# Order of the first loads and of the norm at the head of a transformer block

## The chip, the cores and the metric

The kernel runs on one core of one Trainium2 chip. The metric is the device time of one execution, in microseconds (us). Engines are named as in the profile: PE is TensorE (PEld its weight loads), DVE is VectorE, ACT is ScalarE, POOL is GpSimd, SP is SyncE, which here only issues transfers.

## The reference

One layer of a diffusion backbone over 512 latent tokens with a prefix of 256 context tokens, model width 2048, all in float32. Cut to what matters here:

```python
mod_l = silu(c) @ w_ada + b_ada              # six vectors of 2048 for the latent tokens
mod_c = silu(c_ctx) @ w_ada + b_ada          # the same for the context tokens
h_l = rms_norm(x, g_mix_norm)   * (1 + sc_a)  + sh_a
h_c = rms_norm(ctx, g_mix_norm) * (1 + csc_a) + csh_a
p_l, p_c = h_l @ w_in, h_c @ w_in            # 3904 columns
# p_l: low-rank queries, keys and values, rotary key, three conv streams
# p_c: only keys and values are used
x = x + gt_a * (group_rms_norm(concat(attention, gated_conv)) @ w_out)
x = x + gt_f * conv_ffn(rms_norm(x, g_ffn_norm) * (1 + sc_f) + sh_f)   # 2048 -> 2 x 5504 -> 2048
return rms_norm(x, g_final)
```

rms_norm divides each token's row by the root of its mean square (plus 1e-6) and multiplies by a gain.

## The kernel before, in words

Activations lie transposed: 16 tiles of 128 features by 512 tokens, `xs[0]` to `xs[15]`. Every float32 product is made of three PE matmuls on a high and a low part of weights and activations (`mm3`, L169 to L172): ACT casts the high part, DVE subtracts to get the low one (`split` L145, `hilo` L297).

**The head (L405 to L416).** SP loads constants and the row c. `silu_rows` (L368) takes an 8 KB row on one partition, spreads it over 128 partitions by a PE matmul with ones, four times 512 columns, and ACT writes Silu of it: `sv` for c, `svc` for c_ctx. The 16 tiles of x are loaded; `add_squares` (L310) has ACT square each and DVE add it to one running sum. Then come the row c_ctx in the same way, the small constants `sm` (biases, gains, conv taps), and `rms` (L293): PE sums the squares over the partitions (L283), ACT and DVE make the reciprocal root (L261, L262), PE spreads it (L267), ACT copies it to `rl` (L290).

**Modulation.** One row block of `w_ada` gives 128 outputs: two halves of 512 KB (`ada_load`, four buffers, so two blocks at a time), each multiplied with half of `sv` and summed by DVE (`dot_v` L212, L216), 1.2 us a half. `prep(j)` does blocks 16+j (scale) and j (shift), multiplies tile j by `rl` (L398), scales and shifts it on ACT (L401) and splits it into `hl[j]`.

**The projection (L525 to L569).** It runs over three chunks of the 16 feature tiles, of 2, 4 and 10 tiles. In each chunk the first six column blocks (weights `rf`, matmuls into `pf`) run tile by tile as tiles become ready; the 25 others (weights `rw`, matmuls into `pp`) follow one by one. The first chunk's sums are copied to `acc`, later ones are added. The tiles of the later chunks are prepared between the column blocks of the earlier ones (`todo`). During the third chunk `ctx_mods` uses `svc` for the context's modulation, and `ctx_stats` the context's norm, whose root is ACT's next use of the Sqrt table.

**What sets the order.** The program is put in order by a planner, engine by engine, with its own model of times; each engine then runs its list in that order. `keep(...)` fixes the order among the marked instructions: in the head all loads that go through `fetch_to` (L130) stay in program order on SP's queue until `ordered` is cleared at L548, and so do the multiplies by `rl` among DVE's marked instructions. The write of `sv` to memory (`sv_d`, L910) is not marked, and the planner puts it early. A load whose buffer is still in use waits, and all that stands behind it on SP's queue waits too.

Of the kernel before, what the change touches and what calls it, by code (L numbers as in the profile page):

```python
# [10 lines left out]
F32 = mybir.dt.float32  # L11
F32R = mybir.dt.float32r
AF = mybir.ActivationFunctionType
ALU = mybir.AluOpType
# [3 lines left out]
P = 128  # L18
D = 2048
T = 512  # L20
C = 256
NK = D // P
# [9 lines left out]
G = 6  # L32
# [28 lines left out]
def block_kernel(ctx, tc, xt, ctxt, ctxn, c, c_ctx, w_ada, small, w_in, w_inc, w_q, w_kv, w_out,  # L61
                 w_out_first, w_up, w_up_first, w_dn0, w_dn1, w_dn2, consts, out):
    nc = tc.nc
    keep = tc.keep_in_program_order
    V, A, G_, PE, SP = nc.vector, nc.scalar, nc.gpsimd, nc.tensor, nc.sync
# [18 lines left out]
    def t2(shape, dt, name):  # L84
        return act.tile(shape, dt, tag="t2", bufs=NT2, name=name)
# [44 lines left out]
    def fetch_to(dst, src):  # L130

        ins = SP.dma_start(dst, src)
        if ordered[0]:
            keep(ins)

    def load(src, n, name):
        nth["raw"] += 1
        if "raw" in spare and nth["raw"] % 3 == 0:
            raw = spare["raw"].tile([P, 2048], F32, tag="raw", bufs=1, name=name)
        else:  # L140
            raw = wp.tile([P, 2048], F32, tag="raw", bufs=2, name=name)
        fetch_to(raw[:, :n], src)
        return raw
# [44 lines left out]
    sm = con.tile([P, SMW], F32, name="sm")  # L188
    kc = kcp.tile([P, KCW], F32, name="kc")
    io = con.tile([P, 2 * P], F32, name="io")  # L190
    ident, ones = io[:, :P], io[:, P:]
# [6 lines left out]
    mod = con.tile([P, 96], F32, name="mod")  # L198
    modc = con.tile([P, 32], F32, name="modc")
    rl = con.tile([P, T], F32, name="rl")  # L200
    rc = rl[:, :C]
    sv = svp.tile([P, D], F32, name="sv")
# [9 lines left out]
    def dot_v(raw, vec, t, dst, nm):  # L212

        col = tiny(2, f"dv{nm}{t}")
        for i, r in enumerate(raw):
            V.scalar_tensor_tensor(out=r, in0=r, scalar=1.0, in1=vec[:, i * 1024:(i + 1) * 1024], op0=ALU.mult, op1=ALU.mult, accum_out=col[:, i:i + 1])  # L216
        total(col, t, dst)
# [48 lines left out]
        for g in range(r.shape[1]):  # L266
            PE.matmul(pb[:, g * P:(g + 1) * P], bc(r[:, g:g + 1], P), ident, start=True, stop=True)  # L267

    def rms_steps(sqs, n, a, width, dst, wait=0, one=False):

        ng = width // P
        if not one:
            both = big("rs")
            ps, pb = both[:, :512], both[:, 512:]
        else:
            ps = sml("rs")
            pb = ps[:, 256:]
        for _ in range(wait):
            yield

        for i, sq in enumerate(sqs):
            for g in range(ng):
                PE.matmul(ps[:, g:g + 1], sq[:, a + g * P:a + (g + 1) * P], ones[:, 0:1], start=i == 0 and g == 0, stop=i == len(sqs) - 1 and g == ng - 1)  # L283
        r = tiny(4, "rr")[:, :ng]
        rsqrt(r, ps[:, :ng], n)
        for _ in range(wait):
            yield
        spread(pb, r)
        if dst is not None:
            A.copy(out=dst[:, a:a + width], in_=pb[:, :width])  # L290
        yield pb[:, :width]

    def rms(sqs, n, width, dst):  # L293
        for _ in rms_steps(sqs, n, 0, width, dst):
            pass

    def hilo(src, n, nm, width=512):  # L297
# [12 lines left out]
    def add_squares(total, x, n, nm, E=None, a=0, new=tmp):  # L310
        c = slice(a, a + n)
        if total is None:
            total = new([P, T], F32, nm + "t")
            A.activation(total[:, c], x, AF.Square)
            return total
        q = tmp([P, T], F32, nm)
        A.activation(q[:, :n], x, AF.Square)
        (E or V).tensor_tensor(out=total[:, c], in0=total[:, c], in1=q[:, :n], op=ALU.add)
        return total
# [43 lines left out]
    with ExitStack() as pa:  # L363
        p_sb = pa.enter_context(tc.tile_pool(name="psb", bufs=1, side="right", reuse_waits="tile"))
        svc = p_sb.tile([P, D], F32, name="svc")
        spare["w"] = p_sb, 1, 5

        def silu_rows(src, dst, nm):  # L368

            row = wp.tile([P, 2048], F32, tag="raw", bufs=2, name=nm)[0:1, :]  # L370
            fetch_to(row, src)
            for g in range(4):
                if g % 2 == 0:
                    both = big(f"{nm}{g}")
                ps = both[:, (g % 2) * 512:(g % 2 + 1) * 512]
                PE.matmul(ps, ones[0:1, :], row[:, g * 512:(g + 1) * 512], start=True, stop=True)
                A.activation(dst[:, g * 512:(g + 1) * 512], ps, AF.Silu)

        def ada_load(t):
            return ada_tiles(p_sb, 4, w_ada[t], f"ada{t}")  # L380

        def ada(t):
            dot_v(ada_load(t), sv, t, mod[:, t:t + 1], "l")

        hl = {}

        def mods(j):
            ada(16 + j)
            ada(j)

        def prep(j):
            mods(j)
# [2 lines left out]
        def modulate(j):  # L395

            xr = xs[j]
            keep(V.tensor_tensor(out=xr, in0=xr, in1=rl, op=ALU.mult))  # L398
            sc = tiny(1, f"sc{j}")
            scale_of(sc, s("g_mix", j), mod[:, 16 + j:17 + j])  # L400
            A.activation(xr, xr, AF.Identity, bias=mod[:, j:j + 1], scale=sc)  # L401
            hl[j] = hilo(xr, T, f"h{j}")


        SP.dma_start(io, consts[:, KCW:])  # L405
        silu_rows(c, sv, "c")
        xs = []
        ssq = None
        for j in range(NK):
            xs.append(t2([P, T], F32, f"xr{j}"))  # L410
            fetch_to(xs[j], xt[:, j * T:(j + 1) * T])
            ssq = add_squares(ssq, xs[j], T, f"xs{j}")
        silu_rows(c_ctx, svc, "cc")
        fetch_to(sm, small)
        rms([ssq], D, T, rl)
        A.copy(out=ones_r, in_=ones)  # L416

        qan, kvl, krl, kvc, krc = [], [], [], [], []
# [78 lines left out]
        def evac(ci, m, ps):  # L497
            if ci == 0:
                acc[m] = t2([P, T], F32, f"acc{m}")
                A.copy(out=acc[m], in_=ps)  # L500
                return
            V.tensor_tensor(out=acc[m], in0=acc[m], in1=ps, op=ALU.add)  # L502
            if ci < 2:
                return
            if m == 3:
                bg.appendleft(low_rank([acc[i] for i in range(4)], "g_q", T, "qa", qan))
            elif m == 5:
                bg.appendleft(low_rank([acc[i] for i in (4, 5)], "g_kv", T, "kl", kvl))
            elif m == 6:
                bg.appendleft(rope_key())  # L510
            elif m >= 9 and m % 3 == 0:
                q = bg if m < 27 else post
                q.append(conv((m - 9) // 3))
                q.append(gn_sum((m - 9) // 3, acc[m]))
                late_bg.append(gn_apply((m - 9) // 3, acc[m]))
# [8 lines left out]
        off = 0  # L524
        for ci, (k0, n) in enumerate(zip(K0, KCH)):  # L525

            pss = first_banks(f"pf{ci}")
            if ci == 2:
                bg.append(ctx_stats())
            for q in range(n):  # L530
                if ci == 0:
                    prep(q)
                elif ci == 2:
                    if q in (2, 4):
                        modulate(13 + q // 2)
                    next(cm)
                    pump(1)
                if q % 2 == 0:
                    raw = load(w_in[:, off:off + 2 * G * P], 2 * G * P, f"rf{ci}{q}")
                    w = blocks(raw, 2 * G, f"wf{ci}{q}")  # L540
                    off += 2 * G * P
                for g in range(G):
                    mm3(pss[g], w[q % 2 * G + g], hl[k0 + q], q == 0, q == n - 1)
            for g in range(G):
                evac(ci, ORDER[g], pss[g])
            if ci == 1:
                fetch_to(kc, consts[:, :KCW])
                ordered[0] = False  # L548
            per, step = max(1, 2048 // (n * P)), max(1, 4 // n)
            for i, m in enumerate(ORDER[G:]):  # L550
                if i % per == 0:
                    k = min(per, len(ORDER) - G - i) * n
                    raw = load(w_in[:, off:off + k * P], k * P, f"rw{ci}_{m}")
                    off += k * P
                if i % step == 0:
                    ws = blocks(raw, min(step, len(ORDER) - G - i) * n, f"w{ci}_{m}", i % per * n)
                w = ws[i % step * n:(i % step + 1) * n]
                ps = bank(f"pp{ci}_{m}")
                for kk in range(n):
                    mm3(ps, w[kk], hl[k0 + kk], kk == 0, kk == n - 1)  # L560
                evac(ci, m, ps)
                for f, j in todo.get((ci, i), []):
                    f(j)
                if ci == 2:
                    for q in range(2 if i % 4 == 0 else 1):
                        next(cm, None)
                    if i >= 5 and i % 2 == 1 and (i - 5) // 2 < CTX_EARLY:
                        bg.append(ctx_prep((i - 5) // 2))
                    pump(2)  # L569
# [7 lines left out]
    with ExitStack() as pb:  # L577
# [194 lines left out]
        for n, st in enumerate(steps):  # L772
# [17 lines left out]
            if pr < 3:  # L790
                f, p_, i = pieces(pr + 1)[n % 8]
# [534 lines left out]
```

## Time and profile before

| | us |
|---|---|
| the three times shown | 2206.82, 2209.21, 7098.56 |
| their median | 2209.21 |
| the profiled execution | 2206.8 |
| its span | 2204.9 |
| PE busy in it | 2149.2 (97%) |
| DVE busy | 1599.0 (73%) |
| ACT busy | 1010.5 (46%) |
| first matmul of the projection | starts at 30.24 |

The third of the times stands apart and is a disturbance of that execution. Times in the profile are counted from the start of the span. In a row of the view in order of time stand the start, the time from the first start to the last end, engine, line, operation, what it writes and reads, how many were merged, and in brackets how long the engine stood before it and for whom. SPq is the issue of a transfer, not its landing.

### The profile page before, as it was taken

The numbers are of one execution on the slowest core, as the hardware profiler recorded it, in microseconds if no ns is written. First come the engines' busy times: TensorE is split into PE (matmuls) and PEld (weight loads), VectorE is DVE, ScalarE is ACT, GpSimd is POOL, SyncE is SP. The second block draws the span as 40 slices with busy tenths as digits, with TensorE's granted clock in tenths as the row PEclk, the third lists the DMA queues.
The fourth block names the chain that finished last, engine by engine and source line by source line (L and its number), as shares of the span: only waits on it lengthen the run. The fifth ranks groups of instructions, "written<-read, shape, count | busy, mean of one in ns | idle before, by whom it ended". The sixth has DMA issues, their size and how long they took to land.

```text
span 2204.9 us, 34542 instructions
## 1 busy us (share of the span) xinstructions
PE 2149.2 (97%) x13346; PEld 1914.2 (87%) x13346; DVE 1599.0 (73%) x2493; ACT 1010.5 (46%) x1635; POOL 111.3 (5%) x149
## 2 busy tenths in 40 slices
PE   7899999999999999999999999999999999999998
PEld 4688888878888888899999999999999888888887
DVE  7998887678896848777777777777777873633544
ACT  5523333544452237555554555555554432532444
POOL 0000000000000000011111011111110000000000
PEclk9999999999999999999999999999999999999999
DMA  8989884434469925577777777777776995753462
GB/s 331 344 276 334 275 279 150 144 120 149 158 235 358 331 86 172 132 196 201 204 194 195 201 205 195 194 201 201 201 193 200 350 345 159 247 164 92 160 210 88
DMA packets 144264, 466.75 MB, mean 212 GB/s; under 512 B 16290, under 2 KB 20642, under 8 KB 138082
## 3 DMA queue, kind: packets, MB, share of 16 engines
q1 hardware_dynamic: 125652, 405.03, 54.1%
q0 software_dynamic: 16272, 57.42, 12.8%
q8 instruction: 104, 1.70, 0.3%
q10 hardware_dynamic: 2176, 2.10, 0.3%
q14 instruction: 60, 0.49, 0.1%
HBM read 442.73 MB, written 20.71 MB: 210 GB/s over the span
## 4 chain that ended last, share of the span: by engine, by line
PE 91%; DVE 4%; DMA 2%; ACT 2%; issue 1%; SPq 0%; POOL 0%; DVEq 0%; ACTq 0%
PE d L170 7%; PE d L172 7%; PE d L171 7%; PE pp L170 4%; PE pp L172 4%; PE pp L171 4%; PE o L172 1%; PE o L171 1%; PE o L170 1%; PE uf L170 1%; PE uf L171 1%; PE uf L172 1%; PE of L172 1%; PE pf L171 1%; PE of L170 1%; PE of L171 1%
## 5 line engine op out<-in xcount | busy, mean ns | idle before, releaser
L997 POOL DMA_DIRECT2D u_s<-in_w_up x80 | 68.1, 851 | 416.3 <-DMA u_s<-in_w_up 353.4
L153 ACT CAST w_0h<-rw 128x512 fp32r<-128x512 f32 (+1 forms) x63 | 38.5, 618 | 107.3 <-PE pp L171 65.7
L216 DVE SCALAR_TENSOR_TENSOR ada<-ada,sv 128x1024 f32<-128x1024 f32 x64 | 77.4, 1217 | 4.6 <-DMA ada<-in_w_ada 4.6
L491 DVE SCALAR_TENSOR_TENSOR ada<-ada,svc 128x1024 f32<-128x1024 f32 x64 | 75.9, 1218 | 2.0 <-DMA ada<-in_w_ada 1.8
L238 DVE SCALAR_TENSOR_TENSOR ra<-ra,sv 128x1024 f32<-128x1024 f32 x50 | 59.4, 1216 | 0.0
L154 DVE TENSOR_TENSOR w_0l<-rw,w_0h 128x512 fp32r<-128x512 f32 (+1 forms) x63 | 42.4, 680 | 21.8 <-ACT w_0h L153 21.8
L238 DVE SCALAR_TENSOR_TENSOR ada<-ada,sv 128x1024 f32<-128x1024 f32 x46 | 55.7, 1218 | 2.6 <-DMA ada<-in_w_ada 2.6
L1108 DVE TENSOR_TENSOR u<-u,u 128x1024 f32<-128x1024 f32 x40 | 49.0, 1225 | 1.3
L1107 DVE TENSOR_TENSOR u<-u,u_s 128x1024 f32<-128x1024 f32 x40 | 48.7, 1217 | 0.0
L939 POOL DMA_DIRECT2D y_d<-a x43 | 24.7, 576 | 386.2 <-DVE a L938 376.7
L732 POOL TENSOR_TENSOR gr<-gr,half 128x8 f32<-128x8 f32 x4 | 8.3, 2084 | 641.4 <-DVE mx L684 505.3
L238 DVE SCALAR_TENSOR_TENSOR adl<-adl,sv 128x1024 f32<-128x1024 f32 x32 | 38.8, 1218 | 0.2 <-DMA adl<-in_w_ada 0.2
L683 DVE TENSOR_REDUCE mx<-s 128x1 f32<-128x768 f32 x32 | 30.4, 951 | 8.4 <-PE s L673 8.4
L704 DVE TENSOR_TENSOR ptl<-t,pth 128x384 fp32r<-128x384 f32 x64 | 33.2, 548 | 4.2 <-ACT pth L703 4.2
L502 DVE TENSOR_TENSOR acc<-acc,pp 128x512 f32<-128x512 f32 x50 | 33.9, 678 | 1.9 <-PE pp L172 1.8
L703 ACT CAST pth<-t 128x384 fp32r<-128x384 f32 x64 | 28.5, 488 | 14.3 <-PE t L700 14.1
L936 ACT ACTIVATE g<-g 128x512 f32<-128x512 f32 x43 | 27.2, 633 | 12.1 <-DVE g L930 12.1
L928 ACT ACTIVATE g<-cg,sm 128x512 f32<-128x512 f32 x40 | 32.5, 813 | 0.0
L687 ACT ACTIVATE p<-s,mx 128x768 f32<-128x768 f32 x32 | 29.3, 915 | 6.8 <-DVE mx L684 6.6
L928 ACT ACTIVATE a<-ca,sm 128x512 f32<-128x512 f32 x40 | 32.1, 802 | 0.0
L700 PE MATMUL t<-io,p 128*128 128x128 f32 x192 | 27.5, 274 | 3.7 <-ACT p L687 2.4
L929 DVE SCALAR_TENSOR_TENSOR g<-cg,sm,g 128x511 f32<-128x511 f32 x40 | 29.8, 745 | 0.0
(15580 smaller groups left out, 8734.8 us busy)
## 6 DMA issues: line engine op xcount, KB each, us to landing
ada<-in_w_ada SPq DMA_DIRECT2D x174, 512.0 KB, 6.0
u<-in_w_up SPq DMA_DIRECT2D x120, 512.0 KB, 8.3
u_s<-in_w_up SPq DMA_DIRECT2D x80, 512.0 KB, 4.1
u_s<-in_w_up POOLq DMA_DIRECT2D x80, 512.0 KB, 9.5
d<-in_w_dn SPq DMA_DIRECT2D x86, 384.0 KB, 3.8
y<-y_d SPq DMA_DIRECT2D x129, 256.0 KB, 4.5
ra<-in_w_ada SPq DMA_DIRECT2D x25, 1024.0 KB, 4.8
adl<-in_w_ada SPq DMA_DIRECT2D x32, 512.0 KB, 6.0
```

The lines of the kernel that those rows point to most:

```text
L153: A.copy(out=hi[:, :n], in_=raw[:, a:a + n])
L154: V.tensor_tensor(out=lo[:, :n], in0=raw[:, a:a + n], in1=hi[:, :n].bitcast(F32), op=ALU.subtract)
L170: PE.matmul(ps, w[0], x[0], start=first, stop=False, skip_group_check=on_top)
L171: PE.matmul(ps, w[0], x[1], start=False, stop=False, skip_group_check=on_top)
L172: PE.matmul(ps, w[1], x[0], start=False, stop=last, skip_group_check=on_top)
L216: V.scalar_tensor_tensor(out=r, in0=r, scalar=1.0, in1=vec[:, i * 1024:(i + 1) * 1024], op0=ALU.mult, op1=ALU.mult, accum_out=col[:, i:i + 1])
L238: keep(V.scalar_tensor_tensor(out=r, in0=r, scalar=1.0, in1=svs[i], op0=ALU.mult, op1=ALU.mult, accum_out=lc[:, t % 4:t % 4 + 1] if i else ...
L491: keep(V.scalar_tensor_tensor(out=raw[q], in0=raw[q], scalar=1.0, in1=svc[:, q * 1024:(q + 1) * 1024], op0=ALU.mult, op1=ALU.mult, accum_o ...
L928: A.activation(u, src, AF.Identity, bias=s("fb", m), scale=s("fw", 86 + m))
L997: G_.dma_start(r[-1], src[more], accum_op=ALU.add)
L1107: V.tensor_tensor(out=a11, in0=a11, in1=s1, op=ALU.add)
L1108: V.tensor_tensor(out=a12, in0=a12, in1=a11, op=ALU.add)
```

## The change

Four things move in the head:

- the squares of x are summed by fours: DVE adds within four tiles, and PE sums the four results over the partitions into one accumulator; `rms` takes them one by one as they are made. The number of sums is given as `ns`, since they come from a generator;
- `sm` is loaded before x instead of behind the context's row;
- the context's row is no longer spread by PE: a transfer writes it to all 128 partitions (1 MB instead of 8 KB) after the first chunk's first six column blocks, and ACT takes Silu of it in place, in one pass over 2048 columns, after the second chunk's;
- tile 0's multiplication by `rl` is written right behind the norm, and the first loads are written out: scale block 16, then the first weights `rf00`, then shift block 0. Before, both blocks came ahead of the weights.

```diff
@@ rms_steps, rms
-    def rms_steps(sqs, n, a, width, dst, wait=0, one=False):
+    def rms_steps(sqs, n, a, width, dst, wait=0, one=False, ns=None):
...
-                PE.matmul(ps[:, g:g + 1], sq[:, a + g * P:a + (g + 1) * P], ones[:, 0:1], start=i == 0 and g == 0, stop=i == len(sqs) - 1 and g == ng - 1)
+                PE.matmul(ps[:, g:g + 1], sq[:, a + g * P:a + (g + 1) * P], ones[:, 0:1], start=i == 0 and g == 0, stop=i == (ns or len(sqs)) - 1 and g == ng - 1)
...
@@ ada, modulate
         def ada(t):
-            dot_v(ada_load(t), sv, t, mod[:, t:t + 1], "l")
+            dot_v(first.pop(0) if first else ada_load(t), sv, t, mod[:, t:t + 1], "l")
...
+        def normed(j):
+            keep(V.tensor_tensor(out=xs[j], in0=xs[j], in1=rl, op=ALU.mult))
...
-            keep(V.tensor_tensor(out=xr, in0=xr, in1=rl, op=ALU.mult))
+            if j:
+                normed(j)
@@ the head
         SP.dma_start(io, consts[:, KCW:])
         silu_rows(c, sv, "c")
+        fetch_to(sm, small)
         xs = []
-        ssq = None
-        for j in range(NK):
-            xs.append(t2([P, T], F32, f"xr{j}"))
-            fetch_to(xs[j], xt[:, j * T:(j + 1) * T])
-            ssq = add_squares(ssq, xs[j], T, f"xs{j}")
-        silu_rows(c_ctx, svc, "cc")
-        fetch_to(sm, small)
-        rms([ssq], D, T, rl)
+
+        def squares():
+
+            for j in range(NK):
+                xs.append(t2([P, T], F32, f"xr{j}"))
+                fetch_to(xs[j], xt[:, j * T:(j + 1) * T])
+                ssq = add_squares(ssq if j % 4 else None, xs[j], T, f"xs{j}")
+                if j % 4 == 3:
+                    yield ssq
+
+        rms(squares(), D, T, rl, NK // 4)
+        normed(0)
+        first = [ada_load(16)]
+        first_raw = load(w_in[:, :2 * G * P], 2 * G * P, "rf00")
+        first.append(ada_load(0))
@@ the projection
-                    raw = load(w_in[:, off:off + 2 * G * P], 2 * G * P, f"rf{ci}{q}")
+                    raw = load(w_in[:, off:off + 2 * G * P], 2 * G * P, f"rf{ci}{q}") if off else first_raw
...
             for g in range(G):
                 evac(ci, ORDER[g], pss[g])
+            if ci == 0:
+                fetch_to(svc, c_ctx.to_broadcast([P, D]))
             if ci == 1:
+                A.activation(svc, svc, AF.Silu)
                 fetch_to(kc, consts[:, :KCW])
                 ordered[0] = False
```

More of the change, by code (lines that the diff above doesn't have):

```diff
@@ L291, in rms_steps, with rms @@
         yield pb[:, :width]
-    def rms(sqs, n, width, dst):
-        for _ in rms_steps(sqs, n, 0, width, dst):
+    def rms(sqs, n, width, dst, ns=None):
+        for _ in rms_steps(sqs, n, 0, width, dst, ns=ns):
             pass
```

## The prediction

> **What bounds the kernel now.** I read the page's totals first, then busy time by stage, then the chain of waits in order of time, then each queue's instructions over the first 60 us.
>
> ```profile
> span 2204.9 us, 34542 instructions
> PE 2149.2 (97%) x13346; PEld 1914.2 (87%) x13346; DVE 1599.0 (73%) x2493; ACT 1010.5 (46%) x1635; POOL 111.3 (5%) x149
> 0.00:30.24 30.24, 18.55 (x32) 8.25 (x32) 19.50 (x36) 21.11 (x35) 0.20 (x4) 1.00 0.95 357
> 30.24:82.00 51.76, 45.27 (x174) 33.66 (x174) 45.11 (x91) 25.48 (x47) 0.00 (x0) 1.00 0.88 317
> 82.00:160.00 78.00, 76.64 (x329) 61.69 (x330) 77.00 (x148) 31.46 (x53) 0.00 (x0) 1.00 0.85 305
> 160.00:400.00 240.00, 239.19 (x1071) 194.68 (x1070) 201.75 (x388) 86.58 (x160) 0.00 (x0) 1.00 0.75 254
> ```
>
> The first two lines are the page's, the rest the view of busy time by stage (stretch, length, then PE, PEld, DVE, ACT, POOL, the clock, DMA share, GB/s). PE bounds the kernel: 97% of the span. The change touches only the stretch before PE is saturated. Up to 30.24 us no projection matmul runs at all; from there to 82 us PE misses 6.5 us (51.76 - 45.27) while DVE is 87% busy and DMA 88%; from 82 to 400 us PE misses 2.2 us of 318. So what the change can win is a time by which PE's saturated stretch, starting near 82 us, is moved; PE time taken out before it is worth nothing by itself.
>
> ```profile
> 5.28 5.91 DMA xr<-in_xt
> 11.21 4.29 DMA cc<-in_c_ctx
> 15.64 7.17 PE cc L376 x8
> 23.45 1.28 ACT L261
> 25.27 2.09 PE rs L267 x8
> 28.73 0.82 ACT xr L401
> ...
> 44.58 8.36 DMA rw<-in_w_in
> ...
> 71.29 7.52 DMA ada<-in_w_ada
> 78.83 1.23 DVE ada L216 x2
> 81.51 0.81 ACT xr L401
> ```
>
> The chain of waits (start, length, what). Its first part is the context row: that 8 KB row queues behind x, PE spreads it over the partitions for 7.2 us, and only then comes the sum of squares. Later it runs through loads whose issue waited for a modulation dot to free a buffer (44.58, 71.29), and leaves this stretch at 82 us.
>
> **The norm, step by step.** Rows of ACT, DVE and PE in order of time:
>
> ```profile
> 8.54 11.04 DVE L318 TENSOR_TENSOR xs0t<-xs0t,xs 128x512 f32<-128x512 f32 x14 [1.74 <-ACT xs L317]
> 16.43 0.63 ACT L317 ACTIVATE xs<-xr 128x512 f32<-128x512 f32 x1 [0.17 <-DVE xs0t L318]
> 17.71 0.60 ACT L377 ACTIVATE svc<-cc 128x512 f32<-128x512 f32 x1 [0.65 <-PE cc L376]
> 22.73 1.87 PE L283 MATMUL rs<-io,xs0t 128*128 128x1 f32 x8
> 23.45 1.28 ACT L261 ACT_TABLE_LOAD   x1
> 24.91 0.61 ACT L153 CAST wf_0h<-rf 128x512 fp32r<-128x512 f32 x1
> 28.00 0.69 DVE L398 TENSOR_TENSOR xr<-xr,rl 128x512 f32<-128x512 f32 x1 [0.56 <-ACT rl L290]
> 29.57 0.62 ACT L300 CAST h0h<-xr 128x512 fp32r<-128x512 f32 x1
> 30.24 2.08 PE L170 MATMUL pf<-h0h,wf_0h 128*128 128x512 f32 x4 [2.90 <-ACT h0h L300]
> ```
>
> Squares: ACT ends the last at 17.06, DVE the last add at 19.5 (8.54 + 11.04). By fours there are 12 adds in place of 15, so DVE is no longer behind ACT: 3 x 0.79 = 2.4 us less (11.04 / 14 = 0.79 each). ACT still makes 16 squares. The small constants now load before x: 271 KB, at the 400 GB/s of the rate row below 0.7 us, which I charge in full. Last square 17.06 + 0.7 = 17.8, last add 18.5 (0.7). Three of the four sums on PE lie beside the squares; the last group's 8 records take 1.87, to 20.4. The table load (1.28) starts after the last square, at 17.8, and is covered. Before, the first projection matmul came 5.6 us after that sum (30.24 - 22.73 - 1.87), through root, reciprocal, spread, copy, multiply, affine and cast; the same steps follow now. So by the norm PE starts at 26.0, 4.2 us earlier. The context's matmuls (7.2 us of PE) and its four Silu passes leave this path wholly. The multiply of tile 0 is now written ahead of all dots; what DVE has behind it (the dots, and with them SP's next loads, which wait for their buffers) can stand with it, as it stood 0.56 us at 28.00 before. Bounds: 0.7 us less if the constants cost nothing, 0.7 more if DVE puts half a dot (1.22) between; 25.3 to 26.7.
>
> **The first modulation and weights.** SP's own queue, with time from issue to landing of the three loads of first weights, rf (min/median/max), and of the long weight loads, rw (median), and the rate in slices of 2.5 us from the start:
>
> ```profile
> 15.33 0.33 SPq L132 DMA_DIRECT2D rf<-in_w_in  x1
> 15.96 0.33 SPq L910 DMA_DIRECT2D sv_d<-sv  x1
> 24.93 0.38 SPq L132 DMA_DIRECT2D rw<-in_w_in  x1
> 29.86 14.62 SPq L132 DMA_DIRECT2D ada<-in_w_ada  x8
> 44.58 0.38 SPq L132 DMA_DIRECT2D rw<-in_w_in  x1
> DMA to landing us min/median/max: 8.2/9.0/9.8
> rw<-in_w_in SPq DMA_DIRECT2D x5, 1024.0 KB, 8.4
> GB/s 56 279 302 353 401 395 401 408 429 419 406 424 410 387 354 100 210 226 198 352 374 401 421 411 379 278 283 312 318 156 292 406 420 412 421 395 410 316 306 305
> ```
>
> The first weights were the last of three transfers, issued at 15.33, landing by 24.3 (median 9.0) and cast without a wait at 24.91. Now the shift row's load is last; the bytes up to the end of the three are the same, so its second half lands where the weights did, 23.5 to 24.9, or as early as 22.5 by the rate row (7.5 MB are moved by then, if the write of sv_d keeps behind). Dot 1.22, affine 0.8, cast 0.6: PE at 25.2 to 27.6. The weights' own casts now lie under this. The two paths meet within a microsecond; I take 26.5, a start 3.7 us earlier.
>
> **The context row as a transfer.** The 8 KB load becomes one of 1 MB, and its place in SP's order is behind the second tile's modulation rows and ahead of the first long weight load (rw, issued at 24.93). DMA is full until 37.5 us in the rate row, so 1.05 MB cost 2.6 us at 406 GB/s there: that rw lands at 24.93 + 8.4 + 2.6 = 35.9 instead of 33.3. Rows of ACT and DVE in order of time, and a stretch of the stage view:
>
> ```profile
> 36.28 1.64 ACT L153 CAST w_0h<-rw 128x512 fp32r<-128x512 f32 x3
> 42.90 1.22 DVE L216 SCALAR_TENSOR_TENSOR ada<-ada,sv 128x1024 f32<-128x1024 f32 x1
> 110.00:120.00 10.00, 10.00 (x44) 8.04 (x44) 10.00 (x19) 3.21 (x5) 0.00 (x0) 1.00 0.79 256
> ```
>
> Before, that rw was first cast at 36.28, so it is still just in time: PE meanwhile has the first two tiles' 36 matmuls. Behind it come the four halves for the third tile, 1.3 us each: landing at 37.2, 38.5, 39.8, 41.1, and the last dot ends at 42.3 instead of 44.1 (42.90 + 1.22). That dot frees the way for the second rw in SP's order, the one in the chain at 44.58. So of 3.7 us, 1.8 to 2.0 are sure to get through the transfer, and the hole in the rate row after 37.5 (100 to 226 GB/s, buffers waiting for DVE) takes up the rest of the megabyte. From there to 82 us dots and loads keep their pace and only shift. I take 2.5 us carried, between 1.9 and 3.7.
>
> **Silu of the context, later.** One pass over 2048 columns on ACT, an estimate of 2.4 us (four of 0.60), and two table loads more, to Silu and back for the context's root: 2.6 us (2 x 1.28). Where the program puts it, after the second chunk's first columns near 110 us, ACT is busy 3.2 of 10 us and PE 10.0; the splits queued behind it on ACT have that slack. Nothing, then; 5.0 us if the planner puts it where PE waits for ACT's casts.
>
> The Trainium skill (ScalarE: Activation LUTs, "Rules for kernel authors" and "What ACT_TABLE_LOAD costs") says to do all of one table set before switching, and prices a switch at 2.66 us with its drain; it speaks against this edit, and by it the two would be 5.3 us. The trace has 1.28 and the root right behind the load at 23.45, so the sum goes by 1.28.
>
> Sum, against the profiled execution's own 2206.8 us (span 2204.9 and 1.9 around it): 2206.8 - 2.5 = 2204.3. The median shown, 2209.2, is 2.4 above that execution; the two undisturbed times are these two, and I keep the 2.4 as scatter.
>
> **The rivals.**
> All carried: the hole at 37.5 us swallows the transfer, the whole 4.2 us of the norm path arrives at 82 us and DVE's 2.4 us of adds come on top: 6.6 us, 2200.2. For it: DVE is 87% busy in that stage; against it: the rate row is full until 37.5 and again from 50.
> Nothing carried: DMA runs full from 10 to 37.5 us before and after, so the rows behind the first tile's land no earlier; the hole takes the megabyte, and PE spends the early start waiting for the second and third tile: 2206.8. For it: DMA's 88% over 52 us. Against it: the second tile's dots were not waiting for DMA before.
> Slower: the broadcast reads one row 128 times and is slow at it.
>
> ```profile
> 1.19 0.32 SPq L132 DMA_DIRECT2D c<-in_c  x1
> 3.15 3.75 PE L376 MATMUL c<-c,io 1*128 1x512 f32 x4 [3.15 <-DMA c<-in_c]
> ```
>
> One 8 KB row took 2.0 us from issue to use. Each of 16 DMA engines has eight such rows: 2.6 us if they stream, 16 us if each waits for the one before. Half way, 9.3, is 6.7 more than charged: the first rw lands at 42.6 and PE, out of matmuls near 39, stands: 2204.3 + 6.7 = 2211.0. It decides once the transfer takes over 5.1 us (2.6 + 2.5). [...] No run here shows a row read so often.
> Table switch in the way: the planner sets the Silu before 82 us and ACT's 5.0 us hold up casts: 2204.3 + 5.0 = 2209.3. By the Trainium skill's price of a switch (ScalarE: Activation LUTs, above) it would be an estimated 2212.
> That the change does not do what it says I hold impossible for the row's matmuls: they are gone from the text. The planner's order may hide the rest.
>
> **How the numbers follow.** Forecast 0.50 (2204.3, own range 2203.1 to 2204.9 and 2.4 scatter above), all carried 0.20 (2200.2), nothing 0.15 (2206.8), slow transfer 0.10 (2211.0), switch in the way 0.05 (2209.3). The range takes in the first three with their scatter and the switch, and a reordering of the rest by the planner of 2 us: 2198 to 2210. Two per cent, about what a measurement of this kernel can tell from no change, is 44 us; no case reaches it, so within 2% has 0.97 and each side 0.015.
>
> **What would show it.** The first L170 matmul at 25.2 to 27.6 us; the last square sum on PE ending near 20.4; the second rw issued near 42.6; svc landing within 3 us of its neighbours; PE missing about 4 us between its start and 82. Wrong: a start earlier by 3.7 with the saturated stretch not moved (bytes), or rw cast after 40 us (transfer), or the Silu's table load ahead of 82 us.

## The result, and the profile after

The changed kernel is slower, by a little: 2226.24 us median (2218.10 to 2230.74) against 2211.16 us for the kernel before on the same chip, a ratio of 1.0066 (95% interval 1.0051 to 1.0081). The forecast was 2204.3 us with a range of 2198 to 2210; its sign was wrong and its range too short. The change lies within the 2% that was called most likely.

The profiled execution after took 2218.1 us, span 2216.3 (before: 2206.8 and 2204.9). The page's totals of the kernel after:

```profile
span 2216.3 us, 34561 instructions
PE 2149.1 (97%) x13362; PEld 1921.7 (87%) x13362; DVE 1597.2 (72%) x2490; ACT 1014.2 (46%) x1634; POOL 110.5 (5%) x149
```

PE is as busy as before, 2149.1 us against 2149.2, in a span 11.4 us longer. So the loss is not new work: PE stands 11.5 us more. The medians lie 15.1 us apart (2226.24 - 2211.16), more than the two profiled executions, which are the fastest of their twelve; what follows takes apart the 11.4 us of those two. Busy time by stage, after (columns as in the prediction):

```profile
0.00:28.50 28.50, 17.00 (x48) 11.18 (x49) 17.12 (x31) 18.90 (x31) 0.20 (x4) 1.00 0.94 355
28.50:82.00 53.50, 46.00 (x174) 34.48 (x174) 43.45 (x89) 28.73 (x49) 0.00 (x0) 0.97 0.89 322
82.00:160.00 78.00, 77.10 (x332) 62.54 (x333) 76.95 (x148) 31.25 (x52) 0.00 (x0) 1.00 0.85 305
160.00:400.00 240.00, 237.38 (x1060) 192.68 (x1059) 202.31 (x390) 88.08 (x162) 0.00 (x0) 1.00 0.74 255
900.00:935.00 35.00, 24.17 (x154) 22.37 (x153) 23.62 (x30) 15.46 (x22) 2.52 (x4) 0.85 0.41 103
```

Up to 82 us PE misses 7.5 us (53.50 - 46.00) where it missed 6.5. The last row is of a stage that the change does not touch and the prediction did not look at: from 900 to 935 us, where the FFN's up-projection begins, PE is busy 24.17 of 35 us at a granted clock of 0.85. The same stretch of the kernel before:

```profile
900.00:935.00 35.00, 30.68 (x237) 30.10 (x236) 26.27 (x33) 18.06 (x25) 3.46 (x5) 0.95 0.46 125
```

The starts of the same matmuls in both traces say where the 11.4 us come from. The second kernel-before column is a further execution (e6, below), which shows what two executions of one kernel differ by.

| from, to (first matmul of), in us | before | before again | after | after less before |
|---|---|---|---|---|
| start to third tile of the projection | 84.9 | 85.9 | 84.4 | -0.5 |
| to the third chunk's long columns (`pp` with tile 7) | 130.2 | 130.2 | 130.4 | +0.2 |
| to the scores | 221.2 | 221.3 | 223.1 | +1.9 |
| to the first unbroken row of `of`, the out-projection | 215.8 | 219.0 | 219.7 | +3.9 |
| to `uf`, the up-projection's first columns | 179.8 | 179.7 | 181.2 | +1.5 |
| to `u4a`, past its first products | 87.7 | 87.4 | 93.5 | +5.8 |
| to `u41a`, near the up-projection's end | 737.6 | 737.6 | 737.6 | 0.0 |
| to the end | 547.9 | 545.5 | 546.4 | -1.5 |

So the head, on which the whole forecast rested, gave 0.5 us, and the stages from 215 us on took nearly 12. The chain of waits after, its first part and the one long load that follows:

```profile
13.42 7.82 DMA rf<-in_w_in
23.20 1.14 DVE ada L216 x2
25.55 1.15 DVE ada L216 x2
26.72 5.43 DMA ada<-in_w_ada
32.17 1.25 DVE ada L216 x2
35.13 1.28 ACT L561
36.42 1.91 ACT svc L561
40.77 1.15 DVE ada L216 x2
```

The row's 7.17 us on PE are gone from it, as forecast. The first weights and the dots stand in their place, and then the Silu of the context with its table load, which the prediction had put near 110 us.

### The profile page after: what moved, and what is told of

Its sections match the earlier page's. It is cut to its first block, busy times and chain, and to the rows that moved or that the text cites. A ratio compares the mean times of both kernels' runs of the same rounds, so it can differ in the third digit from the quotient of the medians.

```text
span 2216.3 us, 34561 instructions
## 1 busy us (share of the span) xinstructions
PE 2149.1 (97%) x13362; PEld 1921.7 (87%) x13362; DVE 1597.2 (72%) x2490; ACT 1014.2 (46%) x1634; POOL 110.5 (5%) x149
## 4 chain that ended last, share of the span: by engine, by line
PE 91%; DVE 3%; DMA 3%; ACT 1%; issue 0%; SPq 0%; POOL 0%; DVEq 0%; ACTq 0%
PE d L170 7%; PE d L171 7%; PE d L172 7%; PE pp L170 4%; PE pp L172 4%; PE pp L171 4%; PE o L170 1%; PE o L171 1%; PE o L172 1%; PE of L170 1%; PE of L172 1%; PE of L171 1%; PE uf L170 1%; PE uf L171 1%; PE uf L172 1%; PE pf L170 1%
## 5 line engine op out<-in xcount | busy, mean ns | idle before, releaser
L715 PEld LDWEIGHTS t<-io,p 128*128 128x128 f32 x192 | 22.5, 142 | 9.0 <-ACT p L702 3.4
```

Of the source, the lines that this page charges most:

```text
L715: PE.transpose(tr[:, kb * P:(kb + 1) * P], pt[:, (3 * u + kb) * P:(3 * u + kb + 1) * P], ident)
```

## The experiments

Each kernel computes everything that the reference asks for. The runs came in three groups, each on one chip with its own runs of the kernel before, whose medians were 2212.46 (e1 to e4), 2212.35 (e5 to e8) and 2208.87 us (e9 to e12).

**e1, the row as a transfer alone.** The kernel before, with only this part of the change:

```diff
-        silu_rows(c_ctx, svc, "cc")
...
+            if ci == 0:
+                fetch_to(svc, c_ctx.to_broadcast([P, D]))
             if ci == 1:
+                A.activation(svc, svc, AF.Silu)
```

> The kernel before with one part of the change alone: the context's row is written to all partitions by a transfer behind the first chunk's first columns, and its Silu is one pass on ACT; norm and first loads as before. Theory A (the Silu and its table load stand on ACT right behind tile 1's affine and hold up tile 1's cast): slower than before by 4 to 16 us, with the Silu on ACT before 50 us, as in the changed kernel. Theory B (the 1 MB transfer holds up the loads behind it): also slower by 4 to 16 us, with the weight load behind it landing late. Theory C (the loss is not in the head at all: after 308 us, in stretches where every engine has the same order, PE falls to half clock more often): no fixed sign; the time follows the number of half-clock windows.

Measured: 1.0022 (1.0007 to 1.0038). Slower by about a third of what the whole change costs. The planner puts the Silu early here too (table load at 35.45 us), yet the third tile starts at 83.7 us, 1.2 us earlier than before. What is lost is lost later: 2.8 us up to the scores and 7.8 us in the stage from `uf` to `u4a` (95.5 against 87.7).

**e2, all but the transfer.** The changed kernel with the row spread by PE again, loaded behind x:

```diff
+        for j in range(NK):
+            xs.append(t2([P, T], F32, f"xr{j}"))
+            fetch_to(xs[j], xt[:, j * T:(j + 1) * T])
+        silu_rows(c_ctx, svc, "cc")
...
-            if ci == 0:
-                fetch_to(svc, c_ctx.to_broadcast([P, D]))
...
-                A.activation(svc, svc, AF.Silu)
```

> The changed kernel with the context's row spread by PE again, loaded behind x; the sums by fours, the early constants and the order of the first loads stay. A and B: the loss goes, and 0 to 4 us are won against the kernel before (0.998 to 1.000). C: it may stay as slow as the changed kernel (1.003 to 1.008).

Measured: 1.0061 (1.0036 to 1.0086), as slow as the whole change. That speaks against theories A and B, by which the loss should have gone with the transfer and its Silu. The sum is made up in another way: its head is 5.5 us later than before (third tile at 90.3 us), and its stage from `uf` to `u4a` takes 94.9.

**e4, the sums by fours alone.** The kernel before, with the four sums and the row still ahead of them:

```diff
...
-            ssq = add_squares(ssq, xs[j], T, f"xs{j}")
         silu_rows(c_ctx, svc, "cc")
         fetch_to(sm, small)
-        rms([ssq], D, T, rl)
...
+        def squares():
+            for j in range(NK):
+                ssq = add_squares(ssq if j % 4 else None, xs[j], T, f"xs{j}")
+                if j % 4 == 3:
+                    yield ssq
+        rms(squares(), D, T, rl, NK // 4)
```

> The kernel before with the sums by fours alone; loads in the old order, the row by PE. A and B: 0.999 to 1.001, first projection matmul 0 to 3 us earlier since PE still spreads the context's row ahead of the root. C: may differ from before by up to 0.7% either way.

Measured: 1.0012 (0.9998 to 1.0027). In order of time on PE, e4's head:

```profile
19.59 3.78 PE L376 MATMUL cc<-cc,io 1*128 1x512 f32 x4 [0.54 <-ACT svc L377]
23.30 1.87 PE L283 MATMUL rs<-io,xs0t 128*128 128x1 f32 x8
28.44 1.84 PE L283 MATMUL rs<-io,xs12t 128*128 128x1 f32 x8
30.85 2.08 PE L267 MATMUL rs<-io,rr 128*128 128x128 f32 x8 [0.57 <-DVE rr L262]
35.82 1.65 PE L170 MATMUL pf<-h0h,wf_0h 128*128 128x512 f32 x3 [2.90 <-ACT h0h L300]
```

The sums by fours help only if the row is gone. With the row still on PE the four sums queue behind its matmuls and run one after the other, from 23.30 to 30.28, where one sum took 1.87. The projection starts at 35.82 instead of 30.24. Three of the sums were to lie beside the squares, and they do in the changed kernel; the two edits depend on each other. The expectation, a start 0 to 3 us earlier, had this the wrong way round. Though its third tile comes 5.2 us later than before (90.1 us), the whole kernel is only 0.12% slower, which is not clear of the noise; its stage from `uf` to `u4a` takes 87.1.

**e3, the Silu late.** The changed kernel with the Silu tied behind tile 12's affine, so that it runs at 161.73 us:

```diff
-                A.activation(svc, svc, AF.Silu)
...
+                if (ci, i) == (1, 16):
+                    with tc.issue_after(at[12]):
+                        A.activation(svc, svc, AF.Silu)
```

> The changed kernel with only the Silu of the context's row tied behind tile 12's affine on ACT, near 150 us; the transfer stays where it is. A: the loss goes: 0.998 to 1.001 of before, PE at full clock around 40 us. B: still slow, 1.004 to 1.008. C: as slow as the changed kernel, whatever happens at 35 us.

Measured: 1.0003 (0.9989 to 1.0018), level with the kernel before. This looked like a proof that the early Silu is the loss. The trace speaks against it: the third tile starts at 84.5 us in e3 and at 84.4 in the changed kernel. Putting the Silu off won nothing in the head. The difference lies 800 us later, in the stage from `uf` to `u4a`: 87.7 against 93.5.

**e5, e6, e7: again.** The changed kernel, the kernel before and e1 once more, unedited, to see how far a ratio and a stage's length repeat.

> The changed kernel once more, unaltered. Theory A (its Silu in ACT's way costs it): 1.005 to 1.008 of before again, as on record. Theory D (its instruction order is good, and 1.0066 was the half-clock windows that its executions happened to catch): 0.999 to 1.004. The profile shows whether the half-clock windows fall at the same places as before (39, 452, 480, 644, 913 us).

> The kernel before, unaltered, timed as if it were a changed one: it shows what two identical programs differ by. All theories: 0.9985 to 1.0015. Its profile is a second sample of where PE falls to half clock: D expects other places or another count than the three windows (10 us) of the first profile, since the first was the fastest of its executions.

> The kernel with the context's row by transfer alone, once more. From 78 us on, PE has the same order in it as in the changed kernel. A lasting difference between the two (1.0022 against 1.0066) says that where an execution stands in time decides, not the order; D expects them to meet within 0.002.

Measured: 1.0056 (1.0033 to 1.0078), 1.0004 (0.9985 to 1.0022) and 1.0032 (1.0013 to 1.0050). All three repeat. So does the stage from `uf` to `u4a`: 93.9 in e5, 87.4 in e6, 93.9 in e7. It is a property of the kernel, not of the execution. Theory D, by which 1.0066 was the half-clock stretches that the first executions happened to catch, has this against it: e5 is about as slow again, though its stretches begin at 38, 226, 615, 642, 656 and 912 us and those of the first profile at 39, 452, 480, 644 and 913. Nor does e7 meet e5 within the 0.002 that D asked for, though their intervals overlap.

**e8, transfer and Silu both late.** If transfer and Silu in the crowded head are the loss, this should be the best of all: the transfer goes behind the second chunk's first columns, at 77.45 us, and the Silu is tied as in e3.

```diff
-            if ci == 0:
+            if ci == 1:
+                fetch_to(kc, consts[:, :KCW])
                 fetch_to(svc, c_ctx.to_broadcast([P, D]))
-            if ci == 1:
-                A.activation(svc, svc, AF.Silu)
-                fetch_to(kc, consts[:, :KCW])
...
```

> The changed kernel with the context's transfer moved behind the second chunk's first columns and its Silu behind tile 12's affine. If the 1 MB transfer at 27 us costs the head anything (theory B): 0.997 to 0.999 of before, 1 to 3 us under the version with the Silu alone late (1.0003). If not: 0.999 to 1.002.

Measured: 1.0040 (1.0023 to 1.0057), slower than e3, and its stage from `uf` to `u4a` takes 94.5. The theories that the Silu or the transfer in the head is the loss do not survive this run: with both out of it, 0.4% remains. The head itself behaves as the prediction wanted, in vain. PE's instructions in order of time that ended a wait, of the kernel before, of after, and of e8:

```profile
30.24 2.08 PE L170 MATMUL pf<-h0h,wf_0h 128*128 128x512 f32 x4 [2.90 <-ACT h0h L300]
69.03 0.50 PE L170 MATMUL pp<-h0h,w_0h 128*128 128x512 f32 x1 [0.67 <-ACT acc L500]
```

```profile
28.50 2.07 PE L170 MATMUL pf<-h0h,wf_0h 128*128 128x512 f32 x4 [5.47 <-ACT h0h L300]
68.98 0.50 PE L170 MATMUL pp<-h0h,w_0h 128*128 128x512 f32 x1 [0.68 <-ACT acc L512]
```

```profile
28.25 2.07 PE L170 MATMUL pf<-h0h,wf_0h 128*128 128x512 f32 x4 [5.36 <-ACT h0h L300]
68.89 0.50 PE L170 MATMUL pp<-h0h,w_0h 128*128 128x512 f32 x1 [0.68 <-ACT acc L513]
```

They start 1.7 and 2.0 us earlier than before and stand in step with it at 69 us, within 0.14 us. With the megabyte and the Silu in the head or without them, the start is lost by then.

**What the slow kernels share.** Here is PE at the seam between the `uf` columns and the first products of the up-projection, in order of time. Before:

```profile
901.64 0.40 PE L172 MATMUL uf<-hf15h,ufw15l 128*128 128x512 f32 x1
901.87 0.29 PE L170 MATMUL u3a<-hf0h,u3p1h 128*128 128x256 f32 x1
912.13 0.58 PE L170 MATMUL u3c<-T10h,u3q5h 128*128 128x256 f32 x1 [4.32 <-ACT u3q5h L921]
```

After, with the last DVE and the next ACT instruction that bear on it:

```profile
907.62 0.39 PE L172 MATMUL uf<-hf15h,ufw15l 128*128 128x512 f32 x1
917.94 0.75 DVE L945 SCALAR_TENSOR_TENSOR a<-uf,sm,a 128x511 f32<-128x511 f32 x1
918.84 0.55 PE L170 MATMUL u3a<-hf0h,u3p1h 128*128 128x256 f32 x1 [10.83 <-DVE a L945]
923.87 1.05 ACT L936 CAST u3q5h<-u_s 128x1024 fp32r<-128x1024 f32 x1 [6.75 <-PE u3a L171]
```

Before, the first product `u3a` follows the last `uf` matmul at once, and PE waits later, 4.32 us. After, that same `u3a` waits 10.83 us, until DVE has read the last `uf` sums. `u3a` does not use those sums. It writes into the memory that they lie in. The `uf` sums of the last two column blocks, `uf4`, lie in two of PSUM's eight banks, and the planner chooses which. The banks of the products are a list written out by hand: `BANKS = [0, 1, 7, 4, 5, 6, 2, 3]`, so that `u3a` gets bank 0 and `u3b` bank 1. In the kernels as built, `uf4` begins in bank 2 in before, e3 and e4, and in bank 0 in after, e1, e2 and e8. Those are, without exception, the kernels with 87.1 to 87.7 us in this stage, and those with 93.5 to 95.5.

From 898.7 us (before) and 904.6 us (after) to the end, each engine runs the same instructions in the same order in both kernels. So a bank number is all that sets the seam apart, and it can be changed by itself.

**e9 and e10: the bank alone, both ways.** e9 is the changed kernel with the products moved off `uf4`'s banks; e10 is the kernel before with the products moved onto them. Every engine's instructions and their order stay as they were. e10 swaps only the banks 0 and 1 with 2 and 3; e9's list also deals the other four out in another order.

```diff
-BANKS = [0, 1, 7, 4, 5, 6, 2, 3]
+BANKS = [2, 3, 4, 7, 6, 5, 0, 1]    (e9, on the changed kernel)
+BANKS = [2, 3, 7, 4, 5, 6, 0, 1]    (e10, on the kernel before)
```

> The changed kernel with one line more: the hand-written list of PSUM banks for the up-projection is permuted so that its first two products get banks 2 and 3, which are free in this kernel, instead of 0 and 1, in which the planner left the last wide tile of the stage before. The order of every engine's instructions is the same as in the changed kernel. Theory E (most of the loss is that bank: PE waits some 11 us near 908 us for the last convolution passes to leave it): the stage from the first uf matmul to the first u4a falls from 93.7 to 87.5 us, and the ratio from 1.0056 to 1.0066 down to 1.0025 to 1.0040. Theories A to D: no change.

> The kernel before with the list permuted the other way, so that its first two products get the banks that its last wide tile still holds. Same order of instructions as before. Theory E: the loss appears without any of the change: the stage rises from 87.5 to 93.7 us, ratio 1.0025 to 1.0040. Otherwise 0.9985 to 1.0015.

Measured: e9 1.0031 (1.0015 to 1.0046), e10 1.0041 (1.0025 to 1.0057). The changed kernel sheds half of its loss, and the kernel before gets slower by a number of the same size. PE's wait at the seam in order of time, e9 and then e10:

```profile
908.77 0.29 PE L170 MATMUL u3a<-hf0h,u3p1h 128*128 128x256 f32 x1
919.02 0.58 PE L170 MATMUL u3c<-T10h,u3q5h 128*128 128x256 f32 x1 [4.32 <-ACT u3q5h L936]
```

```profile
908.66 0.39 PE L172 MATMUL uf<-hf15h,ufw15l 128*128 128x512 f32 x1
919.88 0.55 PE L170 MATMUL u3a<-hf0h,u3p1h 128*128 128x256 f32 x1 [10.83 <-DVE a L930]
```

e9 has the wait of before to the last digit, e10 that of after. The difference is 6.51 us (10.83 - 4.32), and the stage's lengths go with it: 87.5 in e9, 95.4 in e10. This cause of the wait, and of about 0.3% of time with it, is shown in both directions.

**e11 and e12: the same mend on e1 and on e8.**

```diff
+BANKS = [2, 3, 4, 7, 6, 5, 0, 1]    (e11, on e1's kernel)
+BANKS = [2, 3, 5, 4, 6, 7, 0, 1]    (e12, on e8's kernel)
```

> The kernel with the context's row by transfer alone (1.0022 and 1.0032) with its bank list permuted as in the changed kernel. E: 0.9985 to 1.0005; the start of the third tile's matmuls stays 1.7 us earlier than before, so if anything keeps, it can come out a little faster than before. Otherwise 1.002 to 1.004.

> The changed kernel with transfer and Silu late (1.0040) and its bank list permuted to its own free banks. E: 1.0000 to 1.0015, level with the version with the Silu alone late (1.0003), whose banks had come out free by chance. Otherwise 1.003 to 1.005.

Measured: e11 1.0016 (0.9999 to 1.0032) and e12 1.0026 (1.0011 to 1.0041), against 1.0022 and 1.0032 for e1 and its repeat, and 1.0040 for e8. The stage is mended in both, 88.9 and 87.7 us, but both ratios lie above what was expected under theory E. They move the right way, by less than the 0.003 that the seam is worth, and their intervals overlap with those of the kernels they mend. By these two alone the mend would not be shown. In e11 the third tile was also expected 1.7 us earlier than before; it came at 86.0 us, 1.1 later, where e1 and its repeat, with the same order of instructions, had 83.7 and 83.6. So one order scatters by 2.4 us at this mark, and the 0.5 us that the changed kernel gained there is less than that.

**What is left.** Mended, the changed kernel is still 0.31% slower than before, 5.6 us (2214.44 - 2208.87). Two places show in the profiles. One is the wait for the attention's last norms ahead of `of`. There the planner fills PE's time with `of` matmuls that are ready. Busy time of the tile `of` alone in the 12.3 us up to the stage's first full row, before and after:

```profile
640.00:652.30 12.30, 5.70 (x21) 3.84 (x22) 0.00 (x0) 1.00 0.86 313
```

```profile
645.50:657.80 12.30, 3.50 (x13) 2.36 (x14) 0.00 (x0) 0.94 0.72 257
```

After, there are 8 fewer (13 against 21); they come behind the wait instead, and 8 at 0.23 us each make 1.8 us, about the 1.5 of the table. e9 has the same 13, and e3, with 25, has the shortest stage. The other is a wait of PE for a weight split near 224 us, in the view of waits of before and then of after:

```profile
PE pp L172 <- DVE w_0l L154: 0.8, 1, 0.8
```

```profile
PE pp L172 <- DVE w_0l L154: 2.1, 1, 2.1
```

After, the planner has one more dot (1.22 us) ahead of that split on DVE. But e10, with the order of before, waited 1.6 us there in one piece. So how much of this is the order's and how much the execution's stays open. Over all fourteen profiles, the stage up to the scores, in which this wait lies, takes 223.1 to 225.9 us in the nine of kernels with the row by transfer and 220.0 to 221.5 in those with the row by PE, but for e10 with 223.1: so some 2 us go with the changed order there, which no run has tried by itself. Stretches at half rate may be a further part (last section). The rest of the 5.6 us stays open too: the attention's stage, 215.8 and 219.0 us in two executions of the kernel before, scatters by more than what is sought. No version was found that beats the kernel before.

## Why the prediction was wrong

**The step that failed: "from there to 82 us dots and loads keep their pace and only shift", and behind it the allowance of "a reordering of the rest by the planner of 2 us".** On the first: PE started 1.7 us earlier where 3.7 was forecast (below), and of that 0.5 was left at the third tile, where 2.5 was forecast; PE missed 7.5 us between its start and 82 us, not about 4. The second was the mis-sized term that decided the sign: the stages which the diff does not touch took nearly 12 us more in the profiled execution, 6.5 of it in one wait that comes of the bank that the planner now chose, the rest in part scatter between executions. The prediction took it that a change in the head can only shift what follows. Here every edit is also an input to a planner, which then deals out orders and PSUM banks for the whole program anew.

**The norm path: right, up to the root.** The last square sum ends on PE at 20.39 (18.52 + 1.87), forecast 20.4; the root starts there. The copy to `rl` then ends at 23.64 us, and the multiply of tile 0, which needs it, starts at 24.87: DVE had a dot and a weight split ahead of it, though the program has it ahead of all dots. Rows of PE, DVE, ACT and SP's queue of the kernel after, in order of time:

```profile
18.52 1.87 PE L283 MATMUL rs<-io,xs12t 128*128 128x1 f32 x8 [0.40 <-DVE xs12t L318]
24.26 0.68 DVE L154 TENSOR_TENSOR wf_8l<-rf,wf_8h 128x512 fp32r<-128x512 f32 x1
24.87 0.68 DVE L392 TENSOR_TENSOR xr<-xr,rl 128x512 f32<-128x512 f32 x1
25.47 1.22 DVE L216 SCALAR_TENSOR_TENSOR ada<-ada,sv 128x1024 f32<-128x1024 f32 x1
26.98 0.81 ACT L405 ACTIVATE xr<-xr,mod,sc 128x512 f32<-128x512 f32 x1 [3.34 <-DVE mod L210]
27.10 0.42 SPq L132 DMA_DIRECT2D svc<-in_c_ctx  x1
35.13 1.28 ACT L561 ACT_TABLE_LOAD   x1
36.42 1.91 ACT L561 ACTIVATE svc<-svc 128x2048 f32<-128x2048 f32 x1
38.87 0.69 DVE L301 TENSOR_TENSOR h1l<-xr,h1h 128x512 fp32r<-128x512 f32 x1 [4.61 <-ACT h1h L300]
38.90 0.86 PE L170 MATMUL pf<-h1h,wf_4h 128*128 128x512 f32 x2 [4.11 <-ACT h1h L300]
47.14 0.38 SPq L132 DMA_DIRECT2D rw<-in_w_in  x1
```

**The modulation path: too early by 0.9 us at the late bound.** PE started at 28.50, forecast 26.5 (25.2 to 27.6). The bytes were not the limit: the shift block's second half landed at 23.8, as forecast, and its dot, the last one, starts at 25.47 with no wait, straight behind a weight split and the multiply by `rl`. I had "the weights' own casts now lie under this"; ACT's casts do, DVE's splits do not, since DVE does them and the dots in one line. The gain at the start was 1.7 us, not 3.7.

**The transfer: right in its price, wrong in its place and effect.** It landed 7.5 us after its issue, within 3 us of the 8.4 of its neighbours and sooner than the weight load issued right behind it, which took 9.7, so the rival of a slow broadcast is out. It was issued at 27.10, with no stall behind it. But the second rw went out at 47.14, where I forecast 42.6 and the kernel before had 44.58. The runs take this apart: 47.14 with transfer and Silu in the head, 45.89 in e3 without the Silu, 43.62 in e8 without either. So the Silu costs that load 1.3 us and the transfer 2.3, close to the 2.6 charged for it. And yet the three of them stand level at the third tile, 84.4, 84.5 and 84.5 us.

**The Silu: its rival came true in place, not in price.** The table load ran at 35.13, ahead of 82 us, which was named as a sign of being wrong. It took the 1.28 of the row that I used, and the pass 1.91, where I had estimated 2.4. Tile 1's cast waited behind it, PE stood 4.11 us and DVE 4.61. Tile 1's matmuls start at 38.90 with it and at 35.18 in e3 without it. The Trainium skill (ScalarE: Activation LUTs, "What ACT_TABLE_LOAD costs") has 2.66 us for the switch, about 1.28 of it the load and the rest a drain. The trace agrees on the load and shows no drain: the pass begins 0.01 us behind the load, and the ACT instruction before the load ends 0.02 us ahead of it. By the time of the third tile it had cost nothing, as e3 shows, so the 5.0 us that the rival charged were not there either.

**Nothing carried (0.15): this is what the head did.** It gave 2206.8; the third tile came 0.5 us earlier and the third chunk's long columns 0.2 (214.8 against 215.1). I gave it too little because I counted against it that the second tile's dots did not wait for DMA before. What paces the head is met later, between 40 and 69 us. Which resource it is, I cannot say from these runs, so the rival's reason, that DMA is full, is not shown though its number was right: e8 took the megabyte away and came to the same 69 us. One more thing shows: behind its wait for tile 1 the changed kernel has 3.4 us of matmuls at half rate from 39.3 us (the clock of 0.97 in its stage row), e3 and e8 have such stretches from 54.6 and 53.9 us, and the three profiles of the kernel before's order have none up to 82 us. Whether these eat the early start, or lie in time that PE would have waited anyway, no run shows.

**All carried (0.20): refuted.** It needed 6.6 us at 82 us, and 0.5 came. DVE's fewer adds and the early start are both lost before 69 us. The head had room for the transfer and the Silu, and gave nothing for what was taken out of it.

## What to carry to other kernels

Where a planner orders the program, a change at its head is not local: look at the whole trace by stage, with the same marks in both kernels, before looking for the cause beside the edit. A list of buffers or banks written out by hand beside buffers that a planner deals out is a trap; check which meet, and change the one number by itself, with the order held, to know its price. And when a run seems to prove a theory, see in its trace whether the gain lies where the theory has it: e3's did not, it came by a bank that fell well by chance.

## What the runs showed of the hardware that I had not expected

**A wait costs more than its length.** A row of the stage view of the kernel after, and one of the mean clock of each of the two profiled executions, before and then after:

```profile
913.40:923.60 10.20, 4.76 (x23) 4.79 (x24) 5.12 (x8) 1.93 (x3) 1.68 (x3) 0.51 0.32 120
```

```profile
core 0: 2204.9 us, clock 0.996
```

```profile
core 0: 2216.3 us, clock 0.992
```

PE stood from 908 to 918.84 us, and then its first 4.8 us of matmuls ran at a granted clock of 0.51, twice as long each. The Trainium skill (TensorE: Matmul & The Clock Gate, "What's actually happening") describes this: half rate after an idle window of about 3.4 us, on a grid that runs by itself. The trace agrees, the half-rate stretch being 10.2 us, three such windows; before, the shorter wait was followed by one. The mean clock falls from 0.996 to 0.992. Over the whole span PE was busy 20.7 us at half rate after, 10.1 before and 16.2 in e6, the kernel before once more. A matmul takes twice its time there (`u3a` 0.55 us after, 0.29 before), so half of these times is lost: an estimated 5.3 us more after than before, and 3.0 us between two executions of one kernel. The changed order has such a stretch near 38 us in all three of its profiles (after, e5, e9) and near 225 us in two, behind the waits there; the kernel before's order has neither in its three (before, e6, e10). Other stretches fall in other places from execution to execution (636, 834 and 912 us before; 477, 614, 641 and 914 in e6), and that may be part of their scatter.

**The same matmuls at the same clock, 1.1% apart.** In the up-projection PE is busy without a gap. The stage view of before and of e9 over the same 725 us:

```profile
935.00:1660.00 725.00, 725.00 (x6112) 725.00 (x6111) 550.86 (x621) 382.24 (x510) 82.35 (x109) 1.00 0.74 199
```

```profile
935.00:1660.00 725.00, 725.00 (x6044) 725.00 (x6044) 543.30 (x613) 377.81 (x504) 81.84 (x108) 1.00 0.74 196
```

Both are full at a clock of 1.00, and one does 6112 matmuls, the other 6044. From `u4a` to `u41a` it is 737.6 us in eleven of the profiles and 745.9 us in three (e5, e9, e12), and e5 is the kernel whose first profile had 737.6. So it goes by the execution, not by the kernel. e9's twelve times fall into seven from 2212.28 to 2215.62 and five from 2219.58 to 2224.09, 9.2 us between their medians, near these 8.3 us; that the two groups are the two rates is not shown, since one of the twelve was profiled. The changed kernel's first twelve times spread as widely, from 2218.10 to 2230.74, and this may be why its median lies further from the kernel before's than its profile does. What makes the difference, no view here shows; differences of this size between two single executions mean nothing.
